# A Mamba-2 layer on one core: most input-projection tiles computed in pairs, by seven half-size products, with weight sums made by accumulating DMA

## The chip, the core and the metric

The kernel runs on one core of one Trainium2 chip. The metric is the device time of one execution, in microseconds (us). TensorE (PE) multiplies matrices, VectorE (DVE) and ScalarE (ACT) do elementwise work, GpSimd (POOL) and SyncE (SP) are used here to issue DMAs. Each engine runs its own instructions in the order in which they stand in the program, and waits where an instruction needs something that another engine or a DMA has not finished.

## What is computed

With DEPTH = 1 the reference is one layer, the Mamba-2 mixer, between two RMSNorms, on 512 tokens of 2048 channels in float32:

```python
proj = rmsnorm(x, ln_g) @ w_in        # 2048 -> 4096 z | 4096 x | 1024 B | 1024 C | 64 dt
z, xbc, dt = split(proj)
xs, bm, cm = split(silu(causal_depthwise_conv(xbc, conv_w, conv_b)))
dt = softplus(dt + dt_bias); a = -exp(a_log)
y = ssd_chunked_scan(xs * dt, dt * a, bm, cm) + d_skip * xs    # 64 heads of 64, 8 groups, state 128
y = rmsnorm(y * silu(z), norm_g) @ w_out
out = rmsnorm(x + y, final_g)
```

## The kernel before

**The input projection.** The 10240 output channels (without dt) are 80 tiles of 128 channels. One tile is a sum over 16 blocks of 128 input channels, for all 512 tokens at once. Weights and x are each split into two float32r parts, hi and lo, and each block takes three matmuls: hi times xh, hi times xl, lo times xh (mm_k, L175 to L179). So a tile is 48 matmuls of 128x512. A tile's weights come in two halves of 512 KB: SP issues the load (load_piece, L72), ACT casts the half to hi (L80), DVE subtracts to get lo (L81). The loaded halves rotate through two buffers ("raw"), the split ones through three ("hi", "lo").

**The order of the work.** The list seq (L102) puts the tiles in order: B and C of a group of heads, then x and z of each "unit" u (two heads, one tile of x and one of z; 32 units, four to a group). PE, SP and here also the events follow the order in which the program writes them; DVE and ACT instructions are put in order by a scheduler when the kernel is built. The scan's work is written as events at fixed steps of the projection, one step for each block of a tile (the tables usual and ramp, L532 to L534): u_load fetches a unit's decay sums, broadcast over 128 partitions, into csb (512 KB); u_decay (L420) makes from them the masked decay matrix m on ACT and DVE; u_xt transposes xs on PE; u_state makes the state of two units; u_yd (L482) multiplies m and x on PE; u_yo (L506) adds the part from the state, multiplies by silu(z) and stores y.

**After a tile.** When an x tile is done, DVE multiplies it by the token's norm into xr (L361), makes the four taps of the convolution (L363, three times L366), and ACT applies SiLU (L368). When a z tile is done, DVE multiplies by the norm (L502) and ACT applies SiLU (L503). The sums are in PSUM tiles named mm, of which there are two, so PE goes on with the next tile while these are read.

**The output projection** (L619 to L722) follows, 1536 matmuls of 128x512; it reads y back from DRAM.

The functions that the change touches:

Of the kernel before, what the change touches and what calls it, by code (L numbers as in the profile page):

```python
# [10 lines left out]
F32 = mybir.dt.float32  # L11
# [4 lines left out]
MANUAL = {mybir.EngineType.PE, mybir.EngineType.SP}  # L16
# [12 lines left out]
EPS = 1e-6  # L29


@with_exitstack
def mamba_layer(ctx: ExitStack, tc: tile.TileContext, d: dict, out: bass.AP):
# [7 lines left out]
    yp0 = ctx.enter_context(tc.tile_pool(name="yp0", bufs=1))  # L41
# [9 lines left out]
    xp = phx.enter_context(tc.tile_pool(name="xhat", bufs=1, side="right"))  # L51
    ps_tr = ph1.enter_context(psum("ps_tr", 2))
    ps_yd = ph1.enter_context(psum("ps_yd", 1))
    ps_yo = ph1.enter_context(psum("ps_yo", 1))
    ps_st = ph1.enter_context(psum("ps_st", 1))
# [16 lines left out]
    def load_piece(src, shape):  # L72
        raw = wp.tile(shape, F32, name="raw", bufs=2)
        nc.sync.dma_start(raw, src)
        return raw

    def split_piece(raw, shape, pool):
        hi = pool.tile(shape, F32R, name="hi")
        lo = pool.tile(shape, F32R, name="lo")
        S.copy(out=hi, in_=raw)  # L80
        V.tensor_tensor(out=lo, in0=raw, in1=hi, op=ALU.subtract)  # L81
        return hi, lo
# [19 lines left out]
    seq = [("B", 0), ("C", 0)]  # L102
    for u in range(NU):
        if u % UPG == 2 and u + 2 < NU:
            seq += [("B", u // UPG + 1), ("C", u // UPG + 1)]
        seq += [("x", u), ("z", u)]
    tile_of = {"z": 0, "x": 32, "B": 64, "C": 72}
    at = {s: i for i, s in enumerate(seq)}
# [9 lines left out]
    NP = 2 * len(seq)  # L118
    pieces = {}

    def w_src(n):
        kind, i = seq[n // 2]
        return d["wi"][tile_of[kind] + i, :, (n % 2) * 8:(n % 2) * 8 + 8, :]

    def get_piece(n):
        if n in pieces or n >= NP + len(wo_order):
            return
        if n < NP:
            pieces[n] = split_piece(load_piece(w_src(n), WSH), WSH, wp)
        else:  # L130
            p, s = wo_order[n - NP]
            pieces[n] = split_piece(load_piece(wo_src(p, s), OSH), OSH, op if n % 4 == 3 else wp)


    xh = [xp.tile([P, L], F32R, name=f"xh{k}") for k in range(KT)]
    xl = [xp.tile([P, L], F32R, name=f"xl{k}") for k in range(KT)]
    xr = sp.tile([P, L + 3], F32, name="xr")

    xbuf = [("csb", 2), ("csb", 2), ("m", 2), ("msh", 1), ("msl", 1)]

    def load_x(k2):
        name, bufs = xbuf[k2 % 5]
        raw = sp.tile([P, 2, L], F32, name=name, bufs=bufs)
# [5 lines left out]
    def split_x(k2, raw):  # L149
        for j in range(2):  # L150
            k = 2 * k2 + j
            S.activation(xh[k], raw[:, j, :], AF.Identity, scale=lng[:, k:k + 1])
            V.scalar_tensor_tensor(out=xl[k], in0=raw[:, j, :], scalar=lng[:, k:k + 1],
                                   in1=xh[k].bitcast(F32), op0=ALU.mult, op1=ALU.subtract)
# [4 lines left out]
    sqbuf = [(n, 2) for n in ("xs", "bc", "y", "z", "csth", "cstl") for _ in range(2)] + \  # L159
        [(n, 1) for n in ("bsl", "bsh")] + [("xd", 2), ("xdth", 2)]  # L160

    def square_x(k2, raw):
        for j in range(2):
            name, bufs = sqbuf[2 * k2 + j]
            sq = sp.tile([P, L], F32, name=name, bufs=bufs)
            S.activation(sq, raw[:, j, :], AF.Square)
            sqs.append(sq)
# [7 lines left out]
    def mm_k(ps, w, k8, k):  # L175
        hi, lo = w
        T.matmul(ps, hi[:, k8, :], xh[k], start=k == 0, stop=False)  # L177
        T.matmul(ps, hi[:, k8, :], xl[k], start=False, stop=False)  # L178
        T.matmul(ps, lo[:, k8, :], xh[k], start=False, stop=k == KT - 1)  # L179


    ps_bc = ps_yd.tile([P, 2, L], F32, name="yd")
    w0, raws, xraw = {}, {}, {}

    def bc_raw(t, half):
        raws[t, half] = wp.tile(WSH, F32, name="raw", bufs=2)
        pool, a, b = (yp0, "yh", "yl") if t and half else (wp, "hi", "lo")
# [570 lines left out]
```

## Time and profile before

| | before |
|---|---|
| median of 3 runs | 1374.59 us (1374.23 to 1374.94) |
| the profiled execution, its time | 1374.24 us |
| its span | 1372.5 us, so 1.7 us lie around the span |
| busy: PE, DVE, ACT, POOL | 1355.7, 876.7, 626.6, 1.7 us |
| DMA: moved, queue of SP and ACT | 170.85 MB, 38.4% of 16 engines' span |

In the page's groups, a row gives line, engine, operation, what is written from what, the shape, the count, then busy time in us, mean ns of one instruction, and the idle time of the engine before them. A matmul's duration contains its way through the array and overlaps the next one, so the distance from one start to the next, in the timeline, is what a matmul costs in a row of them. In the timeline a row is start, duration, engine, line, operation; consecutive equal instructions are merged.

### The profile page before, as it was taken

To read this page: it belongs to the slowest core of one execution; us is meant where nothing else is said; L and a number is where in the kernel's file an instruction comes from. 1 tells how busy PE (TensorE), PEld (TensorE's weight loads), DVE (VectorE), ACT (ScalarE), POOL (GpSimd) and SP (SyncE) were. 2 spreads that over 40 slices of the span, in tenths; PEclk is the share of its full clock that TensorE was granted. 3 is DMA by queue.
4 is the path that set the end of the run, shared out by engine and by line. 5 is a ranking of instruction groups with operands and counts; after the bars stand their busy time and mean duration, and the time that the engine had idled before them with its cause. 6 is when DMAs were issued, how large, how long until landed. Compare 5 with 4: busy or idle time off the path is not lost.

```text
span 1372.5 us, 16466 instructions
## 1 busy us (share of the span) xinstructions
PE 1355.7 (99%) x6388; PEld 1097.1 (80%) x6388; DVE 876.7 (64%) x1433; ACT 626.6 (46%) x894; POOL 1.7 (0%) x11
## 2 busy tenths in 40 slices
PE   7999999999999999999999999999999999999997
PEld 5888878888888888888878888888888888888885
DVE  7867665765666575666557665667647665566545
ACT  7455653635465273546346443736453222223213
POOL 0000000000000000000000000000000000000000
PEclk9999999999999999999999999999999999999998
DMA  7333443523433252434324343424444445454402
GB/s 235 94 113 104 146 126 98 160 58 131 130 112 115 77 158 87 150 100 133 107 77 161 97 134 102 147 92 131 128 146 145 146 152 169 146 163 147 137 30 93
DMA packets 55182, 170.85 MB, mean 124 GB/s; under 512 B 6720, under 2 KB 11136, under 8 KB 54976
## 3 DMA queue, kind: packets, MB, share of 16 engines
q1 hardware_dynamic: 54384, 167.95, 38.4%
q10 hardware_dynamic: 720, 1.84, 0.4%
q8 instruction: 50, 0.82, 0.2%
q14 instruction: 28, 0.23, 0.1%
HBM read 156.99 MB, written 12.78 MB: 124 GB/s over the span
## 4 chain that ended last, share of the span: by engine, by line
PE 97%; DMA 1%; DVE 0%; SPq 0%; ACT 0%; issue 0%; DVEq 0%; ACTq 0%
PE mm L177 21%; PE mm L179 21%; PE mm L178 21%; PE mm L630 9%; PE mm L629 9%; PE mm L631 9%; PE yd L489 2%; DMA raw<-in_wi 1%; PE yd L493 1%; PE tr L456 1%; PE st L477 1%; PE yo L381 0%; PE yo L380 0%; PE yo L382 0%; PE tr L299 0%; PE tr L381 0%
## 5 line engine op out<-in xcount | busy, mean ns | idle before, releaser
L177 PE MATMUL mm<-xh,hi 128*128 128x512 f32 x1248 | 497.1, 398 | 0.0
L179 PE MATMUL mm<-xh,lo 128*128 128x512 f32 x1248 | 489.0, 392 | 0.0
L178 PE MATMUL mm<-xl,hi 128*128 128x512 f32 x1248 | 488.6, 392 | 0.0
L81 DVE TENSOR_TENSOR lo<-raw,hi 128x1024 fp32r<-128x1024 f32 x212 | 258.8, 1221 | 151.8 <-ACT hi L80 151.6
L80 ACT CAST hi<-raw 128x1024 fp32r<-128x1024 f32 x212 | 220.9, 1045 | 262.9 <-PE mm L178 108.6
L179 PEld LDWEIGHTS mm<-xh,lo 128*128 128x128 f32 x1248 | 234.4, 188 | 52.5
L177 PEld LDWEIGHTS mm<-xh,hi 128*128 128x128 f32 x1248 | 234.6, 188 | 51.7 <-issue 5.3
L178 PEld LDWEIGHTS mm<-xl,hi 128*128 128x128 f32 x1248 | 234.7, 188 | 46.2
L630 PE MATMUL mm<-lo,yh 128*128 128x512 f32 x512 | 201.9, 394 | 0.0
L629 PE MATMUL mm<-hi,yh 128*128 128x512 f32 x512 | 201.7, 394 | 0.0
L631 PE MATMUL mm<-hi,yl 128*128 128x512 f32 x512 | 201.7, 394 | 0.0
L629 PEld LDWEIGHTS mm<-hi,yh 128*128 128x128 f32 x512 | 96.2, 188 | 23.2 <-ACT acc L682 0.6
L631 PEld LDWEIGHTS mm<-hi,yl 128*128 128x128 f32 x512 | 96.1, 188 | 22.4
L630 PEld LDWEIGHTS mm<-lo,yh 128*128 128x128 f32 x512 | 96.1, 188 | 22.2
L519 ACT ACTIVATE z<-y 128x512 f32<-128x512 f32 x31 | 19.6, 633 | 123.5 <-DVE y L513 123.5
L686 DVE SCALAR_TENSOR_TENSOR acc<-mm,ry,acc 128x512 f32<-128x512 f32 x72 | 53.4, 747 | 30.5 <-PE mm L631 29.6
L366 DVE SCALAR_TENSOR_TENSOR xs<-xr,par,xs 128x512 f32<-128x512 f32 x96 | 71.8, 748 | 1.4
L436 ACT ACTIVATE m<-csb,cs 128x128 f32<-128x128 f32 x128 | 47.1, 391 | 51.4 <-DMA csb<-cscr 38.1
L442 DVE TENSOR_TENSOR m<-m,cbm 128x512 f32<-128x512 f32 x64 | 44.1, 689 | 38.5 <-ACT m L439 24.2
L368 ACT ACTIVATE xs<-xs 128x512 f32<-128x512 f32 x32 | 20.2, 632 | 69.2 <-DVE xs L366 69.2
L438 DVE TENSOR_SCALAR m<-csb,cs 128x128 f32<-128x128 f32 x128 | 33.7, 280 | 24.5 <-DMA csb<-cscr 24.4
L458 DVE TENSOR_TENSOR xd<-tr,dt 128x512 f32<-128x512 f32 x32 | 22.0, 687 | 31.3 <-PE tr L456 31.3
(211 smaller groups left out, 1173.2 us busy)
## 6 DMA issues: line engine op xcount, KB each, us to landing
raw<-in_wi SPq DMA_DIRECT2D x158, 512.0 KB, 3.9
raw<-in_wo SPq DMA_DIRECT2D x64, 512.0 KB, 4.1
csb<-cscr SPq DMA_DIRECT2D x32, 512.0 KB, 5.8
yscr<-y SPq DMA_DIRECT2D x32, 256.0 KB, 2.3
yr<-yscr SPq DMA_DIRECT2D x16, 512.0 KB, 4.7
ecs<-escr SPq DMA_DIRECT2D x64, 64.0 KB, 5.4
xt<-in_x SPq DMA_DIRECT2D x16, 256.0 KB, 4.6
csb<-in_xT SPq DMA_DIRECT2D x3, 512.0 KB, 8.9
```

The source lines that it names most:

```text
L80: S.copy(out=hi, in_=raw)
L81: V.tensor_tensor(out=lo, in0=raw, in1=hi, op=ALU.subtract)
L177: T.matmul(ps, hi[:, k8, :], xh[k], start=k == 0, stop=False)
L178: T.matmul(ps, hi[:, k8, :], xl[k], start=False, stop=False)
L179: T.matmul(ps, lo[:, k8, :], xh[k], start=False, stop=k == KT - 1)
L366: V.scalar_tensor_tensor(out=ca, in0=xr[:, k:k + L], scalar=convw[:, t, k:k + 1], in1=ca, op0=ALU.mult, op1=ALU.add)
L436: S.activation(o, l, AF.Relu, scale=-1.0, bias=b)
L442: V.tensor_tensor(out=ma[:, i], in0=ma[:, i], op=ALU.mult, in1=cbm[:, i, 0:2, :].rearrange("p b l -> p (b l)").unsqueeze(1).to_broadcast([ ...
L629: T.matmul(ps, yh, hi, start=k == 0, stop=False)
L630: T.matmul(ps, yh, lo, start=False, stop=False)
L631: T.matmul(ps, yl, hi, start=False, stop=k == n - 1)
L686: V.scalar_tensor_tensor(out=a, in0=ps, scalar=ry[:, t:t + 1], in1=a, op0=ALU.mult, op1=ALU.add)
```

## The change

Four pairs of tiles (B and C of group 0, x and z of units 0 and 1, B and C of group 1) stay as they were. The other 36 pairs, p = x or B and q = z or C, are computed together, by a scheme of Winograd's kind with seven products in place of eight. The two tiles' weights are four halves by input channels; x is four quarters, by input channels and by tokens. A product is 8 blocks of three matmuls of 128x256 (product, L584), so a pair takes 168 matmuls of 128x256 in place of 96 of 128x512.

- **Weights.** Four halves are loaded as before (R11, R12, R21, R22). Four sums are made by DMAs that POOL issues and that add a half from DRAM onto a half in the chip's memory (q_add, L558): T1 is made on top of R11, T2 on top of T1, T4 on top of T2, all three in one buffer ra; T3 on top of R12 in buffer rb. Each sum can start when the split of what stood there has been read by ACT and DVE. All seven are split into hi and lo by ACT (L81) and DVE (L82), R11 into buffers of its own (h1h, h1l), the other six through three buffers. R21 and R22 use two buffers rc.
- **x.** Four sums of quarters of x are made once, on the chip: three forms in x_forms from a second load of x, in buffers s0 to s11, and one in x_form3 over the second half of the tokens of the first 8 blocks.
- **Products of a pair** (pair, L595), in order: R11 into S, T4 of the pair before into A, T1 into R, R21 into A, T2 onto S, R22 onto R, T3 onto S. S and R are PSUM tiles, of which a pair uses one half and the next pair the other. A is the tile of p; the tile of q comes out of S and R with sign changed. Between products ACT copies S or R away (L605, L609, L612, L617), and DVE adds the copies to R and S for z (L614, L616). T4's product, written in the next pair, ends p; then DVE does norm and convolution as before (L374, L365, three times L368).
- **The units.** Their events now stand at 28 steps to a pair, a step for every 6 matmuls. m and csb have one buffer in place of two, xd too. u_decay makes all its sums on ACT (8 Relu and 4 Exp of 128x128, one Exp of 128x1024) and one product on DVE (L436, 128x1536). The state is made unit by unit by two float32 matmuls (L462) in place of six float32r ones for two units; B, C and the scan's mask are no longer split where they make the decay's mask (L408, L409: float32).

```diff
+    NPL = 8
...
+    QS = 28
...
+        m = sp.tile([P, 2, 6, P], F32, name="m")
...
-                for o, l, b in ((ma[:, i, hh, 0:P], la, cs[:, 2 * i, h:h + 1]),
...
-                    if i == 0:
-                        S.activation(o, l, AF.Relu, scale=-1.0, bias=b)
-                    else:
-                        V.tensor_scalar(out=o, in0=l, scalar1=b, scalar2=0.0, op0=ALU.subtract, op1=ALU.min)
...
+                S.activation(m[:, i, hh, :], la, AF.Relu, scale=-1.0, bias=cs[:, 2 * i, h:h + 1])
+                S.activation(m[:, i, 2 + hh, :], lb, AF.Relu, scale=-1.0, bias=cs[:, 2 * i + 1, h:h + 1])
+                S.activation(m[:, i, 4 + hh, :], lb, AF.Exp, bias=nwl[:, 2 * i, h:h + 1])
+        S.activation(m[:, :, 0:4, :], m[:, :, 0:4, :], AF.Exp, scale=-1.0)
+        m6 = m.rearrange("p c (b h) l -> p (c b) h l", h=2)
+        V.tensor_tensor(out=m6, in0=m6, op=ALU.mult,
+                        in1=cbm.rearrange("p c b l -> p (c b) l").unsqueeze(2).to_broadcast([P, 6, 2, P]))
...
-        xd = sp.tile([P, NC, 2, HD], F32, name="xd", bufs=2)
+        xd = sp.tile([P, NC, 2, HD], F32, name="xd")
...
-        pst = ps_st.tile([P, 4 * HD], F32, name="st")
...
-        terms = [(Bt[0], xw[0]), (Bt[0], xw[1]), (Bt[1], xw[0])]
+        pyo = ps_yo.tile([P, 3, P], F32, name="yo")
...
         for c in range(2):
-            for i, (a, b) in enumerate(terms):
-                T.matmul(pst, a[:, c, :], b[:, c].rearrange("p u h d -> p (u h d)"), start=c + i == 0, stop=c + i == 3)
-        st = split(pst, [P, 4 * HD], "sts")
...
+            T.matmul(pyo[:, 2, :], Bt[:, c, :], xw[:, c].rearrange("p h d -> p (h d)"), start=c == 0, stop=c == 1)
+        un[u]["sts"] = split(pyo[:, 2, :], [P, P], "sts")
+        un[u]["pyo"] = pyo
...
+            S.copy(out=hi, in_=t)
+            V.tensor_tensor(out=lo, in0=t, in1=hi, op=ALU.subtract)
+
+        V.tensor_tensor(out=t1, in0=n2[:, :, hi_], in1=n1[:, :, hi_], op=ALU.subtract)
+        V.scalar_tensor_tensor(out=t2, in0=t1, scalar=-1.0, in1=n1[:, :, lo_], op0=ALU.mult, op1=ALU.subtract)
+        put(1, t1)
+        V.scalar_tensor_tensor(out=t1, in0=t2, scalar=-1.0, in1=n2[:, :, lo_], op0=ALU.mult, op1=ALU.subtract)
+        put(2, t2)
+        put(4, t1)
+
...
+    def q_split(n, f, own=False):
+        raw = qs[n][f]
+        qs[n, f] = split_piece(raw, WSH, wp, *((("h1h", "h1l"), 1) if own else ()))
...
+    def q_add(n, f, old, half, tile_):
+
+        raw = qs[n][old]
+        nc.gpsimd.dma_start(raw, w_half(quads[n][tile_], half), accum_op=ALU.add)
+        qs[n][f] = raw
...
+    def q_events(n):
+        b = NPL * KT + n * QS
+        for o, f, a in ((-34, q_load, ("R11", 0, 0, "ra")), (-15, q_split, ("R11", True)),
+                        (-15, q_add, ("T1", "R11", 0, 1)), (-2, q_split, ("T1",)),
+                        (-2, q_add, ("T2", "T1", 1, 1)), (13, q_split, ("T2",)),
+                        (13, q_add, ("T4", "T2", 1, 0)), (24, q_split, ("T4",)),
+                        (-7, q_load, ("R12", 0, 1, "rb")), (-6, q_add, ("T3", "R12", 1, 1)),
+                        (21, q_split, ("T3",)),
+                        (-10, q_load, ("R21", 1, 0, "rc")), (1, q_split, ("R21",)),
+                        (2, q_load, ("R22", 1, 1, "rc")), (17, q_split, ("R22",))):
+            add(b + o, f, n, *a)
...
+    def product(ps, w, f, first, step):
...
+        for k in range(KH):
+            if k % 2 == 0:
+                run(step + k // 2)
+            hi, lo = w()
+            ah, al = operand(f, k)
+            T.matmul(ps, hi[:, k, :], ah, start=first and k == 0, stop=False, skip_group_check=True)
+            T.matmul(ps, hi[:, k, :], al, start=False, stop=False, skip_group_check=True)
+            T.matmul(ps, lo[:, k, :], ah, start=False, stop=k == KH - 1, skip_group_check=True)
...
+    def pair(n, prev):
...
+        A = ps_mm.tile([P, L], F32, name="mm")
+        s_, r_ = [x[:, (n % 2) * LH:(n % 2) * LH + LH] for x in SR]
...
+        product(s_, W("R11"), 11, True, b)
+        S.copy(out=A[:, lo_], in_=s_)
+        if prev:
+            prev(b + 4)
+        product(r_, W("T1"), 1, True, b + 8)
+        S.copy(out=sn[:, 1, :], in_=r_)
+        product(A[:, lo_], W("R21"), 12, False, b + 12)
+        product(s_, W("T2"), 2, False, b + 16)
+        S.copy(out=sn[:, 0, :], in_=s_)
+        product(r_, W("R22"), 4, False, b + 20)
+        V.tensor_tensor(out=zq[:, lo_], in0=r_, in1=sn[:, 0, :], op=ALU.add)
+        product(s_, W("T3"), 3, False, b + 24)
+        V.tensor_tensor(out=zq[:, hi_], in0=s_, in1=sn[:, 1, :], op=ALU.add)
+        S.copy(out=A[:, hi_], in_=s_)
...
+            V.tensor_tensor(out=zq, in0=zq, in1=rbc, op=ALU.mult)
+            S.activation(zq, zq, AF.Silu, scale=-1.0)
...
+        def last(step):
+            product(A[:, hi_], W("T4"), 22, False, step)
+            normed(A)
+            (g_b if kp == "B" else u_x)(ip)
...
+    ramp = [[57, 62, 54, 73, 84, 90], [48, 57, 48, 66, 82, 88]]
...
+        w = ramp[u] if u < len(ramp) else [24, 38, 50, 58, 61, 66]
+        for o, f in zip(w, (u_load, u_decay, u_xt, u_state, u_yd, u_yo)):
+            add(at["x", u] + o, f, u)
...
+    nc = bacc.Bacc("TRN2", target_bir_lowering=False, num_devices=1, dynamic_dma_scratch_size=1024)
```

**Order, PE at the seam of two tiles or pairs.** Before, the end of one tile (xh_121 is the last block of x) and the start of the next; names in brackets are the semaphores of the engines waited for:

```order
L380 MATMUL yo<-csth,stsh 128x256 [waits DVE_49]
L381 MATMUL yo<-cstl,stsh 128x256
L382 MATMUL yo<-csth,stsl 128x256
L177 MATMUL mm<-xh_121,hi 128x512
L178 MATMUL mm<-xl_137,hi 128x512
L179 MATMUL mm<-xh_121,lo 128x512
L177 MATMUL mm<-xh_106,hi 128x512
L178 MATMUL mm<-xl_122,hi 128x512
L179 MATMUL mm<-xh_106,lo 128x512
```

Now, the end of T3's product and the start of the next pair's R11 product, both in S:

```order
L592 MATMUL S<-xl,hi 128x256
L593 MATMUL S<-xh,lo 128x256
L591 MATMUL S<-xh,hi 128x256
L592 MATMUL S<-xl,hi 128x256
L593 MATMUL S<-xh,lo 128x256
L591 MATMUL S<-xh,h1h 128x256 [waits Activation_49]
L592 MATMUL S<-xl,h1h 128x256
L593 MATMUL S<-xh,h1l 128x256
L591 MATMUL S<-xh,h1h 128x256
L592 MATMUL S<-xl,h1h 128x256
L593 MATMUL S<-xh,h1l 128x256
```

Before, the next tile starts here with no wait of its own. Now the first matmul of the next pair waits for an ACT instruction, the copy L617 of the sum that has just ended.

**Order, ACT around the end of a pair.** Before, the stretch around a z tile (L503); L368 and L439 belong to the same and the next unit:

```order
L439 ACT_TABLE_LOAD
L439 ACTIVATE m<-m 128x768
L440 ACTIVATE m<-m 128x768
L80 CAST hi<-raw 128x1024
L368 ACT_TABLE_LOAD
L368 ACTIVATE xs<-xs 128x512
L80 CAST hi<-raw 128x1024 x2
L503 ACTIVATE z<-z 128x512
L466 CAST xwsh<-xw 128x2x128
L374 CAST stsh<-st 128x256
L80 CAST hi<-raw 128x1024
```

Now, the splits of T4, of the next pair's T1 and R21 (ra, ra, rc), then the copy L617 that PE waits for, SiLU of z and the split of the state:

```order
L612 COPY sn<-S 128x256
L81 CAST hi<-ra 128x1024 x2
L81 CAST hi<-rc 128x1024
L617 COPY mm<-S 128x256
L623 ACTIVATE z<-z 128x512
L379 CAST stsh<-yo 128x128
L81 CAST h1h<-ra 128x1024
L605 COPY mm<-S 128x256
```

Where before only a weight split and SiLU stood, a copy that PE waits for now stands behind three weight splits, and the first two of these read what accumulating DMAs have written.

**Order, DVE from the end of an x tile to the next weight split.** Before:

```order
L361 TENSOR_TENSOR xr<-mm,rbc 128x512
L438 TENSOR_SCALAR m<-csb,nwl 128x128
L363 TENSOR_SCALAR xs<-xr,par 128x512
L81 TENSOR_TENSOR lo<-raw,hi 128x1024
L366 SCALAR_TENSOR_TENSOR xs<-xr,par,xs 128x512
L438 TENSOR_SCALAR m<-csb,cs 128x128
L366 SCALAR_TENSOR_TENSOR xs<-xr,par,xs 128x512
L438 TENSOR_SCALAR m<-csb,cs 128x128
L366 SCALAR_TENSOR_TENSOR xs<-xr,par,xs 128x512
```

Now, from the end of T4's product (L374) to the split of T2 (L82 lo<-ra):

```order
L374 TENSOR_TENSOR xr<-mm,rbc 128x512
L365 TENSOR_SCALAR xs<-xr,par 128x512
L368 SCALAR_TENSOR_TENSOR xs<-xr,par,xs 128x512
L492 TENSOR_TENSOR ecs<-yo,ecs 128x256
L368 SCALAR_TENSOR_TENSOR xs<-xr,par,xs 128x512
L493 TENSOR_TENSOR y<-y,ecs 128x256
L368 SCALAR_TENSOR_TENSOR xs<-xr,par,xs 128x512
L494 TENSOR_TENSOR y<-y,z 128x512
L436 TENSOR_TENSOR m<-m,cbm 128x1536
L82 TENSOR_TENSOR lo<-ra,hi 128x1024
```

Before, a weight split stands fourth. Now all of the convolution, the unit's y (L492 to L494) and the whole decay product (L436) stand ahead of the split of T2.

More of the change, by code (lines that the diff above doesn't have):

```diff
@@ L29 @@
 EPS = 1e-6
+KH = KT // 2
+LH = L // 2
 @with_exitstack
@@ L598, in mamba_layer @@
     add(b0 + 56, dt_spread)
-    for n in range(2, len(seq)):
+    for n in range(2, NPL):
         ps = None
@@ L614, in mamba_layer @@
             finish(n, ps)
+    prev = None
+    SR = [ps_q.tile([P, L], F32, name=x) for x in ("S", "R")]
+    for n in range(len(quads)):
+        prev = pair(n, prev)
+    prev(END)
     phx.close()
-    assert NP + 3 not in pieces
     op = ctx.enter_context(tc.tile_pool(name="op", bufs=1, side="right"))
     acc = [op.tile([P, DM], F32, name=f"acc{t}") for t in range(NC)]
-    step = len(seq) * KT
+    step = END + 4
     def mm_o(ps, blk, w, t):
```

314 lines of the change are left out of this document (169 added, 145 removed).

## Prediction

> **What bounds the kernel now.** I read the page first: the busy times and the chain that ended last.
>
> ```profile
> PE 1355.7 (99%) x6388; PEld 1097.1 (80%) x6388; DVE 876.7 (64%) x1433; ACT 626.6 (46%) x894; POOL 1.7 (0%) x11
> PE 97%; DMA 1%; DVE 0%; SPq 0%; ACT 0%; issue 0%; DVEq 0%; ACTq 0%
> ```
>
> PE is busy for 99% of the span and is 97% of the chain. Then the waits, for PE alone:
>
> ```profile
> PE yd L177 <- ACT xh L152: 6.4, 1, 6.4
> PE yd L178 <- DVE xl L153: 1.1, 3, 0.6
> ```
>
> These are all: 7.5 us, at the start. Every result of DVE, ACT and DMA is there before PE wants it. So a matmul fewer is time gained, as long as that stays so; and a wait that PE gets is time lost in full. Third, the timeline of PE, for what a matmul costs in a row of them: 21 matmuls of 128x512 between the first two rows, six of 128x256 between the next three.
>
> ```profile
> 600.59 0.40 PE L177 MATMUL mm<-xh,hi 128*128 128x512 f32 x1
> ...
> 605.40 0.39 PE L177 MATMUL mm<-xh,hi 128*128 128x512 f32 x1
> ...
> 662.48 0.28 PE L477 MATMUL st<-xwsh,bth 128*128 128x256 f32 x1
> ...
> 663.07 0.28 PE L477 MATMUL st<-xwsh,btl 128*128 128x256 f32 x1
> ...
> 663.19 0.40 PE L177 MATMUL mm<-xh,hi 128*128 128x512 f32 x1
> ```
>
> A 128x512 costs 4.81 / 21 = 0.2290 us. The last of the six 128x256 starts at 663.07 and the next matmul at 663.19, so one costs 0.71 / 6 = 0.1183 us: a little more than half.
>
> **Part 1, the products.** 36 pairs had 36 x 96 = 3456 matmuls of 128x512, 791.4 us. They get 36 x 168 = 6048 of 128x256, 715.5 us. Gain: 75.9 us, not the eighth (98.9) that the count of products promises, since the half-size matmul is dearer by its share. The Trainium skill's page "TensorE: Matmul & The Clock Gate" (Back-to-back issue gap) gives N/2.4 + 2.5 ns, 216 and 109 ns; by that the gain would be 85 us. The trace has 229 and 118 ns, and decides.
>
> **Part 2, the scan on PE.** The state took six 128x256 for two units, 0.71 us. It takes four float32 128x128. For these the nearest row is L275, four such matmuls in eight records:
>
> ```profile
> L275 PE MATMUL tr<-z,ones x8: 270/275/276, 45.3 to 46.1; 128*128 128x128 f32 x8
> 642.09 0.28 PE L380 MATMUL tr<-csth,bsh 128*128 128x256 f32 x1
> 643.42 0.45 PE L177 MATMUL mm<-xh,hi 128*128 128x512 f32 x1
> 631.03 0.60 PE L456 MATMUL tr<-ident,xs 128*128 128x128 f32 x4
> 631.39 0.48 PE L177 MATMUL mm<-xh,hi 128*128 128x512 f32 x1
> ```
>
> 0.8 / 7 is 0.114 us a record, 0.23 a matmul, 0.91 for two units: 0.2 more, 16 times, +3.3 us. The decay's mask took twelve matmuls, 1.33 us from 642.09 to 643.42; two float32 of 256 and two of 128 columns come to 2 x (0.46 + 0.23) = 1.37: nothing. The four transposes of xs keep their 0.36 us.
>
> **Part 3, the split of T2 behind the decay.** Prices on DVE and ACT, from the groups (mean ns behind the busy time):
>
> ```profile
> L81 DVE TENSOR_TENSOR lo<-raw,hi 128x1024 fp32r<-128x1024 f32 x212 | 258.8, 1221 | 151.8 <-ACT hi L80 151.6
> L80 ACT CAST hi<-raw 128x1024 fp32r<-128x1024 f32 x212 | 220.9, 1045 | 262.9 <-PE mm L178 108.6 <-PE mm L631 92.8 <-DMA raw<-in_wi 34.6
> L361 DVE TENSOR_TENSOR xr<-mm,rbc 128x512 f32<-128x512 f32 x46 | 31.5, 685 | 15.2 <-PE mm L179 15.0
> L363 DVE TENSOR_SCALAR xs<-xr,par 128x512 f32<-128x512 f32 x32 | 17.4, 544 | 0.6
> L366 DVE SCALAR_TENSOR_TENSOR xs<-xr,par,xs 128x512 f32<-128x512 f32 x96 | 71.8, 748 | 1.4
> L511 DVE TENSOR_TENSOR ecs<-yo,ecs 128x256 f32<-128x256 f32 x32 | 13.5, 421 | 30.1 <-PE yo L382 30.0
> L512 DVE TENSOR_TENSOR y<-y,ecs 128x256 f32<-128x256 f32 x32 | 13.4, 420 | 0.6
> L513 DVE TENSOR_TENSOR y<-y,z 128x512 f32<-128x512 f32 x32 | 22.0, 688 | 0.6
> L442 DVE TENSOR_TENSOR m<-m,cbm 128x512 f32<-128x512 f32 x64 | 44.1, 689 | 38.5 <-ACT m L439 24.2 <-ACT m L440 14.1
> L436 ACT ACTIVATE m<-csb,cs 128x128 f32<-128x128 f32 x128 | 47.1, 391 | 51.4 <-DMA csb<-cscr 38.1 <-PE tr L382 9.2 <-PE mm L178 4.1
> L439 ACT ACT_TABLE_LOAD x27 | 34.6, 1283 | 0.5
> L439 ACT ACTIVATE m<-m 128x768 f32<-128x768 f32 x32 | 27.1, 845 | 0.3
> L374 ACT CAST stsh<-st 128x256 fp32r<-128x256 f32 x16 | 5.9, 371 | 50.0 <-PE st L477 50.0
> ```
>
> And how instructions follow each other, from the timeline:
>
> ```profile
> 610.56 0.85 ACT L439 ACTIVATE m<-m 128x768 f32<-128x768 f32 x1
> 611.32 1.98 ACT L80 CAST hi<-raw 128x1024 fp32r<-128x1024 f32 x2
> 611.44 0.69 DVE L442 TENSOR_TENSOR m<-m,cbm 128x512 f32<-128x512 f32 x1 [0.23 <-ACT m L439]
> 612.72 1.22 DVE L81 TENSOR_TENSOR lo<-raw,hi 128x1024 fp32r<-128x1024 f32 x1
> 613.85 0.74 DVE L366 SCALAR_TENSOR_TENSOR bc<-xr,par,bc 128x512 f32<-128x512 f32 x1
> ```
>
> An engine that waited starts 0.03 us after the end it waited for (610.56 + 0.85 = 611.41, L442 at 611.44). Instructions that don't need each other overlap by 0.09 (L81 would end at 613.94, the next starts at 613.85). Two weight casts take 1.98, so a cast follows after 0.94.
>
> When T4's last matmul starts, call it 0; it ends at 0.28 (the length of a 128x256 above), and DVE starts L374 at 0.31. In the new order ten instructions end with T2's lo: 0.685 + 0.544 + 3 x 0.748 + 0.421 + 0.420 + 0.688 + 1.75 + 1.221 = 7.97 us. (1.75 is L436 on 1536 elements: 0.689 for 512, 1.221 for 1024, so 0.53 for each further 512.) Seven overlaps take 0.63 off, two dependent starts add 0.06: 7.4 us, so lo is there at 7.75. PE meanwhile has T1's 24 matmuls, 3 for the state's part of y, R21's 24, and two of T2 that want only hi: it wants lo at 54 x 0.1183 = 6.39. **It waits 1.36 us a unit; 30 units, +40.8 us.** ACT's line to the same split is level: from the end of the unit's y on PE, 12 x 0.368 (47.1 / 128) + 1.28 + 1.06 (1024 elements) + 0.37 + 1.05 = 8.2 us, against 69 matmuls, 8.2 us. I add nothing for it.
>
> **Part 4, the seam between pairs.** Call the start of T3's last matmul 0. R21's cast waits for the matmul before it and starts at -0.12 + 0.28 + 0.03 = 0.19. L617 stands behind it: 1.13. It takes 0.37 (as L374), so PE may go on at 1.53; it could have at 0.12. **1.41 us at each of 35 seams, +49.4 us.** Were no cast in front, the line over L616 on DVE (as L511) would still give 0.31 + 0.42 + 0.03 + 0.37 + 0.03 = 1.16, a wait of 1.04, +36.4 us. The copies L605, L609 and L612 cost nothing: at least 24 other matmuls (2.84 us) stand between a product and the next use of its half of S, R or A, and 0.31 + 0.37 hides there.
>
> **Part 5, the adds.** No accumulating DMA and no DMA of POOL is in the trace. The nearest rows:
>
> ```profile
> q1 hardware_dynamic: 54384, 167.95, 38.4%
> raw<-in_wi SPq DMA_DIRECT2D x158, 512.0 KB, 3.9
> csb<-cscr SPq DMA_DIRECT2D x32, 512.0 KB, 5.8
> ```
>
> 167.95 MB in 38.4% of 1372.5 us is 319 GB/s, 1.64 us for 512 KB of data; 2.26 of the 3.9 us are not data. POOL issues T4's add when T2's lo is there, and the next pair's T1 add right behind it. T1's cast stands ahead of R21's cast and L617, so it has to start 0.94 us before R21's can. PE has from T2's third matmul 22 + 24 + 24 matmuls and the transposes, 8.64 us; so T1 must have landed within 7.7 us or the seam gets longer by all that it is late. Lower bound, adds like loads: 3.9 + 1.64 = 5.5, no cost. Upper bound: three times the data (read two, write one), 2.26 + 2 x 4.92 = 12.1. I take twice the data, since an add reads two sources where a load reads one: 2.26 + 2 x 3.28 = 8.8, and 0.8 for half of a load of SP (R21's, 1.64) among it: 9.6, late by 1.9. **35 x 1.9 = +66.5 us.** The Trainium skill's page "Collectives: The Full Stack" (the bandwidth ceiling) says this of adds by DMA: both sources go through one read ring, so a reduce runs at half a copy's rate; no run here shows it. That is the rule that speaks against this change.
>
> SP's R11 load waits for T4's lo, and behind it are csb and R22. csb's 5.8 us have until the next unit's decay, which waits for the unit's y on PE, over 6 us after T3: covered, barely. DMA's share: 144 adds of 3.28 us on 527 make 1000 us of some 1465, 68%: no bound.
>
> **Part 6, the forms of x.** DVE gets 40 instructions of 0.7 us, 28 us, in the stage that has the least room:
>
> ```profile
> 50.00:150.00 100.00, 100.00 (x482) 81.31 (x482) 77.20 (x142) 53.59 (x82) 0.00 (x0) 1.00 0.32 104
> ```
>
> DVE had 23 us idle of 100 there. I add 8, between 0 (spread) and 16.
>
> **The sum**, against the profiled span: 1372.5 - 75.9 + 3.3 + 40.8 + 49.4 + 66.5 + 8 = 1464.6; with the 1.7 us around it, 1466.3. The profiled execution took 1374.24, the median is 1374.59: the same for this purpose. About 0.2% (2.7 us) can be told from no change.
>
> **The rivals.**
>
> 1. *The adds land in time* (0.22). Then Part 5 is 0: 1399.8 us. For it: the loads' 5.5 us are under 7.7. The Trainium skill's "DMA: Bandwidth & Descriptors" (Anatomy of one DMA) has 2.0 us + bytes/436 GB/s for a DMA of GpSimd, an estimated 3.2 us for 512 KB, and so this time.
> 2. *The adds are slow* (0.13): with three times the data and the same 0.8, T1 lands after 12.9, 5.2 late: +182 in place of +66.5, 1581.8 us. Nothing in the profile excludes it.
> 3. *Faster* (0.12): DVE's line before T2 is hidden (it would have to end 1.4 us sooner, by more overlap), the adds are in time, and a seam costs only 1.04: 1372.5 - 75.9 + 3.3 + 36.4 + 8 + 1.7 = 1346.0 us. It decides from a total wait under (75.9 - 3.3 - 8) / 35 = 1.85 us a pair. Against it: Parts 3 and 4 alone sum to 2.6, from rows.
> 4. *Waits and gain cancel* (0.03).
>
> **How the numbers follow.** My forecast has 0.50; rivals 0.22, 0.13, 0.12, 0.03. Faster 0.12, same 0.03, slower 0.85. The range 1385 to 1580 holds the forecast and rival 1 with the bounds of Parts 5 and 6, and about half of rival 2; some 0.2 is outside.
>
> **What would show it.** In the profile after: matmuls of the products 0.118 us apart; waits of PE for ACT L617 of about 115 us in all (50 if the adds are in time) and for DVE L82 of about 40; POOL's adds 5 to 8 us from issue to landing; PE busy near 90%. Waits of PE under 65 us in all would make it wrong towards faster; adds over 10 us, towards rival 2; a PE that waits for ACT L81 more than for L617 would mean that the casts, not the seam, are the bound.

## The result, and the profile after the change

The changed kernel takes **1574.79 us** (median of 4 runs, 1569.62 to 1575.99), the kernel before 1374.72 in the same rounds: 1.1449 times as long, interval 1.1422 to 1.1475. The forecast was 1466.3 us in a range of 1385 to 1580. The sign and the range held; of the loss of 200 us the forecast had 92.

The page of the profile after, from the parts that were shown of before:

```profile
span 1567.9 us, 22414 instructions
PE 1355.0 (86%) x8980; PEld 1224.6 (78%) x8980; DVE 983.6 (63%) x1333; ACT 787.8 (50%) x1291; POOL 126.5 (8%) x155
q0 software_dynamic: 20736, 75.51, 26.6%
DMA 40%; PE 28%; issue 16%; DVE 9%; ACT 6%; POOL 1%; SPq 0%; POOLq 0%; ACTq 0%; DVEq 0%
```

PE was 97% of the chain that ended last; now DMA is 40% of it and PE 28%. PE's busy time is the same as before (1355.7), though the matmuls have 76 us less to do: that is the first sign that they ran slower. The mean clock granted to PE is 0.949 of full speed, before it was 0.997. POOL's adds, a median from issue to landing in the last column:

```profile
ra<-in_wi POOLq DMA_DIRECT2D x108, 512.0 KB, 8.5
```

The waits (in total, times, longest): PE's, which were 7.5 us in all before, and ACT's casts, which wait for the adds:

```profile
PE S L591 <- ACT mm L617: 106.5, 35, 5.8
PE S L593 <- DVE lo L82: 40.0, 30, 2.9
PE tr L408 <- DVE xd L450: 21.1, 7, 3.1
ACT hi L81 <- DMA ra<-in_wi: 192.9, 73, 3.9
```

With the smaller ones PE's sum to 203.3 us.

One seam, from the timelines of POOL, ACT, DVE and PE:

```profile
616.44 0.86 POOL L561 DMA_DIRECT2D ra<-in_wi  x1 [0.91 <-DVE h1l L82]
624.14 1.04 ACT L81 CAST hi<-ra 128x1024 fp32r<-128x1024 f32 x1 [2.85 <-DMA ra<-in_wi]
625.10 1.04 ACT L81 CAST hi<-rc 128x1024 fp32r<-128x1024 f32 x1
626.81 0.36 ACT L617 COPY mm<-S 128x256 f32<-128x256 f32 x1 [0.68 <-DVE z L616]
625.22 1.22 DVE L82 TENSOR_TENSOR lo<-ra,hi 128x1024 fp32r<-128x1024 f32 x1 [1.41 <-ACT hi L81]
626.36 0.42 DVE L616 TENSOR_TENSOR z<-S,sn 128x256 f32<-128x256 f32 x1
623.74 0.28 PE L593 MATMUL S<-xh,lo 128*128 128x256 f32 x1
627.22 0.58 PE L591 MATMUL S<-xh,h1h 128*128 128x256 f32 x1 [3.20 <-ACT mm L617]
627.60 0.41 PE L592 MATMUL S<-xl,h1h 128*128 128x256 f32 x1
627.82 0.41 PE L593 MATMUL S<-xh,h1l 128*128 128x256 f32 x1
...
630.65 0.28 PE L592 MATMUL S<-xl,h1h 128*128 128x256 f32 x1
630.77 0.28 PE L593 MATMUL S<-xh,h1l 128*128 128x256 f32 x1
```

T1's add is issued at 616.44 and lands 7.7 us later. Its cast, R21's cast and T1's lo follow, L616 stands on DVE behind that lo, L617 behind L616, and PE goes on at 627.22, after 3.2 us. That is the forecast's seam. What the forecast didn't have is behind it: the matmuls come 0.21 us apart where 0.12 is usual, until 630.2. The windows of the same stretch (PE, weight loads, DVE, ACT and POOL busy, then the granted clock):

```profile
626.00:628.00 2.00, 0.78 (x3) 0.78 (x4) 1.97 (x4) 0.95 (x3) 1.50 (x2) 0.71 0.86 251
628.00:630.00 2.00, 2.00 (x12) 2.00 (x11) 0.64 (x1) 0.17 (x1) 0.00 (x0) 0.50 0.97 305
630.00:632.00 2.00, 2.00 (x18) 2.00 (x18) 0.29 (x1) 0.27 (x1) 0.00 (x0) 0.94 1.08 241
```

Half the clock from about 626.8 until 630.2 (0.71 and 0.94 are windows that hold both), so for some 3 us of PE's work: 12 matmuls in 2 us where 18 follow in the next two.

How much that is in all: the forecast's terms without any wait give 1372.5 - 7.5 - 75.9 + 3.3 + 8 = 1300.4 us, the **base**. With the 203.3 us of waits that is 1503.7. The span is 1567.9. The **rest**, 64.2 us, is in neither matmuls at full pace nor waits. An estimate from PE's rows alone agrees: this trace has 153.6 us at half clock amid its work, and the distances between matmuls there exceed the usual ones by 64 us in all. The theory to test (A): the waits have the causes that the forecast named, and behind a wait of several us PE's clock is halved, which costs the rest. The rivals: the rest comes from the products or the adds' traffic (B); or the adds are no cause at all and only the order on ACT is.

### The profile page after: what moved, and what is told of

It reads as the page before. It is cut to its first block, busy times and chain, and to the rows that moved or that the text cites. A ratio compares the mean times of both kernels' runs of the same rounds, so it can differ in the third digit from the quotient of the medians.

```text
span 1567.9 us, 22414 instructions
## 1 busy us (share of the span) xinstructions
PE 1355.0 (86%) x8980; PEld 1224.6 (78%) x8980; DVE 983.6 (63%) x1333; ACT 787.8 (50%) x1291; POOL 126.5 (8%) x155
## 3 DMA queue, kind: packets, MB, share of 16 engines
q0 software_dynamic: 20736, 75.51, 26.6%
## 4 chain that ended last, share of the span: by engine, by line
DMA 40%; PE 28%; issue 16%; DVE 9%; ACT 6%; POOL 1%; SPq 0%; POOLq 0%; ACTq 0%; DVEq 0%
DMA ra<-in_wi 34%; PE mm L750 7%; PE mm L751 7%; PE mm L749 7%; DVE lo L82 4%; ACT hi L81 3%; DMA rb<-in_wi 3%; DMA csb<-cscr 1%; DVE xs L368 1%; DMA ra<-in_wo 1%; POOL ra L561 1%; PE mm L180 1%; PE mm L181 1%; PE mm L182 1%; PE S L591 1%
## 5 line engine op out<-in xcount | busy, mean ns | idle before, releaser
L81 ACT CAST hi<-ra 128x1024 fp32r<-128x1024 f32 x168 | 176.1, 1048 | 342.2 <-DMA ra<-in_wi 192.9
L82 DVE TENSOR_TENSOR lo<-ra,hi 128x1024 fp32r<-128x1024 f32 x168 | 205.1, 1222 | 204.8 <-ACT hi L81 200.2
L591 PE MATMUL S<-xh,h1h 128*128 128x256 f32 x288 | 104.5, 363 | 106.5 <-ACT mm L617 106.5
L591 PE MATMUL mm<-xh,hi 128*128 128x256 f32 x576 | 163.7, 284 | 2.2 <-ACT mm L617 2.2
L593 PE MATMUL R<-s,lo 128*128 128x256 f32 x576 | 161.1, 280 | 2.9 <-DVE lo L82 2.9
L591 PE MATMUL R<-s,hi 128*128 128x256 f32 x576 | 163.4, 284 | 0.0
L593 PE MATMUL mm<-xh,lo 128*128 128x256 f32 x576 | 160.4, 278 | 3.4 <-DVE lo L82 3.4
L592 PE MATMUL mm<-xl,hi 128*128 128x256 f32 x576 | 160.6, 279 | 0.0
L592 PE MATMUL R<-s,hi 128*128 128x256 f32 x576 | 160.4, 278 | 0.0
L591 PEld LDWEIGHTS mm<-xh,hi 128*128 128x128 f32 x576 | 108.2, 188 | 7.2 <-issue 4.8
L591 PEld LDWEIGHTS R<-s,hi 128*128 128x128 f32 x576 | 108.2, 188 | 0.0
L592 PEld LDWEIGHTS R<-s,hi 128*128 128x128 f32 x576 | 108.2, 188 | 0.0
L592 PEld LDWEIGHTS mm<-xl,hi 128*128 128x128 f32 x576 | 108.1, 188 | 0.0
L81 ACT CAST hi<-rc 128x1024 fp32r<-128x1024 f32 x76 | 79.2, 1042 | 39.3 <-PE S L592 25.2
```

The lines of the kernel that those rows point to most:

```text
L591: T.matmul(ps, hi[:, k, :], ah, start=first and k == 0, stop=False, skip_group_check=True)
L592: T.matmul(ps, hi[:, k, :], al, start=False, stop=False, skip_group_check=True)
L593: T.matmul(ps, lo[:, k, :], ah, start=False, stop=k == KH - 1, skip_group_check=True)
```

## The experiments

Below, the rest of a run is its span less 1300.4 less the sum of PE's waits.

### Plain loads for the adds

```
-        nc.gpsimd.dma_start(raw, w_half(quads[n][tile_], half), accum_op=ALU.add)
+        nc.gpsimd.dma_start(raw, w_half(quads[n][tile_], half))
```

> The 144 adds of POOL become plain loads of the same 512 KB from the same queue at the same places (the sums of weights are not made: the products take the second tile alone). Theory A (the adds are late, and PE's clock falls after waits of several us): a load of 512 KB takes 5 to 6 us instead of 8.5, so T1 lands in time; PE's wait for L617 falls from 106 to about 50 us, that for L408 and L593 stays, and of the 70 us of lowered clock some 20 go: about 1494 us. Rival B (the adds cost nothing at the seam, the order of casts on ACT does): L617's wait stays above 95 us, 1560 to 1575 us.

Measured: **1457.23 us** (1.0603, 1.0585 to 1.062), clock 0.986. PE's waits, and then POOL's DMAs on the page:

```profile
PE S L591 <- ACT mm L617: 55.6, 35, 2.9
```

```profile
q0 software_dynamic: 20736, 75.51, 15.1%
ra<-in_wi POOLq DMA_DIRECT2D x108, 512.0 KB, 5.3
```

L617's wait falls from 106.5 to 55.6: the late adds are 50.9 us of it, the seam by itself 55.6. The waits are 130.8 us in all, 72.5 less than with adds, but the time is 118 less: the rest falls from 64.2 to 18.4 us with it (1449.6 - 1300.4 - 130.8). So A was right on the wait, and its time is 37 us too long: more of the lost clock came back than it had. No wait at L617 is over 3 us any more. Of the 35 seams, 21 now wait 1.29 us, the least that any has; with the adds 12 wait 1.29 to 1.39, and 20 wait 2.4 to 5.8: the adds make some seams much longer and others not at all. The same 75.51 MB take 15.1% of 1449.6 us, 345 GB/s; as adds 26.6% of 1567.9, 181 GB/s.

### S and R change roles from pair to pair

```
-        s_, r_ = [x[:, ...] for x in SR]
+        s_, r_ = [x[:, ...] for x in SR[::1 - n % 2 * 2]]
```

> S and R change roles from pair to pair, so that the next pair's R11 goes to the tensor that L614 has read long before, and no longer waits for L617; T4 of the pair before wants L617 24 matmuls (2.84 us) later. Theory A: of 106.5 us behind L617 (35 waits, 3.0 each) some 15 stay, in front of T4's first matmul; the clock is lowered less, by some 35 us: 1445 us. Rival B (the late add of T1 sets the pace, whatever waits for it): the wait moves to T4 or T1 nearly whole, over 80 us of it, 1545 us or more.

Measured: **1484.23 us** (1.0802, 1.0786 to 1.0818), clock 0.967. All of the computation is kept.

```profile
PE tr L408 <- DVE xd L450: 21.9, 7, 4.2
PE R L593 <- DVE lo L82: 21.0, 20, 1.3
PE S L593 <- DVE lo L82: 19.0, 19, 1.5
PE R L591 <- ACT hi L81: 13.9, 4, 5.9
PE mm L591 <- ACT mm L617: 9.4, 9, 2.4
```

Of L617's 106.5 us, 9.4 stay, so the late copy mattered mainly because the very next product wanted the tensor that it reads. Some of the wait moved: R11's product now waits 14.1 us for L614, and T2's 23.2 for its cast (L81), which was 5.6. The time is 39 us over what A expected: the waits that are left sum to 138.0, with 5.9 and 4.2 us among the longest, and the rest is still 43.2.

### Waits put into the kernel before

This is the test of the clock by itself: the kernel before, all of its work, and two small POOL instructions that the first matmul of a tile must wait for.

```
+    def hold(src, w):
+        dl = sp.tile([P, 1], F32, name="dl", bufs=2)
+        Q.tensor_scalar(out=dl, in0=src[:, 0:1], scalar1=0.0, scalar2=1.0, op0=ALU.mult, op1=ALU.add)
+        Q.tensor_tensor(out=w, in0=w, in1=dl, op=ALU.mult)
...
+            if n > 9 and k == 0 and seq[n - 1][0] == "x":
+                hold(un[seq[n - 1][1]]["xs"], pieces[2 * n][0][:, 0, 0:1])
```

In a first form the two POOL instructions were copies that didn't need each other.

> The kernel before, all of its work, with 29 to 32 waits added: the first matmul after each x tile waits for a POOL copy that waits for the unit's x (conv and silu), some 5 us. Theory A (the clock falls after such waits): the granted clock falls from 0.997 to 0.95 or less, matmuls after a wait are over 0.3 us apart for some us, and the span grows by clearly more than the waits, by 30 to 80 us. Rival B (the lowered clock of the changed kernel comes from its products or its traffic): clock 0.99 or more, and the span grows by the waits alone, to within 10 us.

> As the one with long waits, but the first matmul after each z tile waits for the gate z (one instruction of DVE and one of ACT), some 2 us. Theory A (only waits of several us lower the clock): clock 0.99 or more, the span grows by the waits alone. Theory C (any wait of PE lowers it): clock under 0.98, and the span grows by the waits and 20 us or more.

These two tell nothing of it: the scheduler put the second copy ahead of the first, and PE waited for neither. They took 1386.59 and 1388.23 us at a clock of 0.998. In the form above:

> The kernel before with all of its work, and 29 waits of PE added: the first matmul of the tile behind an x tile waits for two small POOL instructions, and these for the unit's x (conv and silu on DVE and ACT), some 5 us; this time the second POOL instruction needs the first one's result, so that the scheduler can't put it ahead. Theory A (the granted clock falls after a wait of 2.5 us or more, and 1.5 to 3 us are lost behind each): clock 0.96 or less, and the span grows by the waits and 45 to 90 us more. Rival B (the lowered clock comes from the products or the traffic of the adds): clock 0.99 or more, and the span grows by the waits to within 10 us.

> The same behind z tiles, where the two POOL instructions wait for the gate z, one instruction of DVE and one of ACT, so about 2 us. Theory A (a wait under 2 us costs 0.3 to 0.5 us beside itself, a longer one 1.5 and more): clock 0.98 or more, and the span grows by the waits and some 10 to 20 us. Rival C (any wait lowers the clock alike): clock and added time as with the long waits.

> The kernel before with the waits behind the gate z, but at the third k of the tile, two k steps (1.4 us) later, so that 117.6 us of waits become some 75, most of them 1.2 to 1.6 us. Theory A (under 2 us the clock stays): clock 0.98 or more, no more than 15 us beside the waits themselves. Rival C (any wait of this kind costs 1.6 us beside itself): 45 us beside the waits.

Measured, one run each: **1641.51 us** behind x, **1539.02** behind z, **1482.78** behind z two steps later; clock 0.930, 0.961, 0.977. PE's waits for POOL in the three, in this order:

```profile
PE mm L177 <- POOL hi L526: 202.6, 29, 10.3
```

```profile
PE mm L177 <- POOL hi L526: 117.6, 29, 7.0
```

```profile
PE mm L177 <- POOL hi L526: 77.1, 29, 5.8
```

The spans grew by 267.3, 164.8 and 108.6 us, so by 64.7, 47.2 and 31.5 more than these waits: 2.2, 1.6 and 1.1 us a wait. Some 5 us of each surplus are not the clock: a wait is counted from the end of the last matmul's record (0.39 us), while without a wait the next one would start 0.23 us after its start, so each of the 29 costs 0.16 us more than is counted. No product was changed and no add was there, so B falls. A's numbers held behind x alone: behind z it had 10 to 20 us (the waits are 4.1 us on the mean, not 2), and two steps later 15 at most. Then waits of different length, first one of the third kernel and after it three of the second, each with the matmuls behind it:

```profile
723.68 0.50 PE L177 MATMUL mm<-xh,hi 128*128 128x512 f32 x1 [1.33 <-POOL hi L526]
724.02 0.40 PE L178 MATMUL mm<-xl,hi 128*128 128x512 f32 x1
724.26 0.39 PE L179 MATMUL mm<-xh,lo 128*128 128x512 f32 x1
```

```profile
672.04 0.50 PE L177 MATMUL mm<-xh,hi 128*128 128x512 f32 x1 [2.70 <-POOL hi L526]
672.38 0.40 PE L178 MATMUL mm<-xl,hi 128*128 128x512 f32 x1
672.62 0.39 PE L179 MATMUL mm<-xh,lo 128*128 128x512 f32 x1
...
608.84 0.51 PE L177 MATMUL mm<-xh,hi 128*128 128x512 f32 x1 [2.70 <-POOL hi L526]
609.18 0.40 PE L178 MATMUL mm<-xl,hi 128*128 128x512 f32 x1
609.42 0.50 PE L179 MATMUL mm<-xh,lo 128*128 128x512 f32 x1
609.72 0.63 PE L177 MATMUL mm<-xh,hi 128*128 128x512 f32 x1
610.14 0.63 PE L178 MATMUL mm<-xl,hi 128*128 128x512 f32 x1
...
723.69 0.80 PE L177 MATMUL mm<-xh,hi 128*128 128x512 f32 x1 [3.59 <-POOL hi L526]
724.28 0.63 PE L178 MATMUL mm<-xl,hi 128*128 128x512 f32 x1
724.71 0.63 PE L179 MATMUL mm<-xh,lo 128*128 128x512 f32 x1
```

Behind 1.33 us the matmuls are 0.24 apart from the second on. Behind 3.59 they are slow at once (0.59 from the first start to the second, then 0.43 apart). Behind two waits of the same 2.70 us it goes both ways. Read so over the stretch from 200 to 1160 us of these two kernels: the 15 waits of 1.33 to 2.2 us lost 0.5 us or less behind them; of 14 of 2.5 to 2.7 us eight lost 1.3 to 2.0 and six nothing; of the 23 longer ones all but one lost 1.6 to 3.1, no more for 7 us than for 4. So rival C, that any wait costs alike, falls too.

But the length of a wait doesn't decide it by itself. Ahead of that stretch a wait of 2.15 us (second kernel, at 142 us) and one of 2.29 us (third kernel, at 169 us) lost 1.3 and 1.7 us. What decides is in the clock that the traces record. In every trace here it changes only at moments that are whole steps of 3.41 us apart. These are the windows of the second kernel cut at those moments, around the two waits of 2.70 us that end at 608.84 and 672.04 (length, PE, weight loads, DVE, ACT and POOL busy, then the clock):

```profile
606.15:609.56 3.41, 0.72 (x3) 0.62 (x4) 2.52 (x5) 1.75 (x3) 1.02 (x2) 1.00 0.00 0
609.56:612.97 3.41, 3.41 (x10) 2.64 (x9) 0.00 (x0) 0.00 (x0) 0.00 (x0) 0.50 0.00 0
...
667.58:671.00 3.42, 1.76 (x10) 1.14 (x8) 2.25 (x4) 1.81 (x3) 0.11 (x1) 1.00 0.14 56
671.00:674.41 3.41, 2.37 (x10) 1.99 (x11) 0.94 (x2) 0.09 (x1) 0.90 (x2) 1.00 0.01 2
674.41:677.82 3.41, 3.41 (x19) 2.91 (x18) 0.00 (x0) 0.00 (x0) 0.00 (x0) 1.00 0.00 0
```

The first wait lies whole in one step, and the next step is at half clock. The second is cut by the end of a step into 1.66 and 1.04 us, and no fall comes. Counted over every step of full clock in the changed kernel and in the second and third kernel here (the first 12 and the last 15 us left out): each of the 66 falls comes after a step with 1.7 us of waiting or more, and none of the 1156 other steps has over 1.9. Two waits in one step add up. In the changed kernel one of 0.88 and one of 0.85 us were enough:

```profile
903.31:906.72 3.41, 1.68 (x13) 1.27 (x12) 3.41 (x4) 2.44 (x3) 0.00 (x0) 1.00 0.02 2
906.72:910.13 3.41, 3.41 (x16) 3.41 (x17) 3.41 (x4) 3.38 (x5) 1.70 (x2) 0.50 0.43 55
```

So PE's clock is halved for the next step when about half of a step was idle. In the three kernels a fall lasts one step or two; a wait over 2.5 us often fills half a step, and one of 1.33 us can't by itself.

The Trainium skill's page "TensorE: Matmul & The Clock Gate" (Part 1: The HAM clock gate) describes this: a gate halves PE's clock when PE was idle over a window of about 3.4 us, the window runs freely, and while the gate is down matmuls of 512 columns are 426.7 ns apart. The 0.43 agrees, and so does the window that runs freely: steps of 3.41 us, and equal waits that go both ways. That PE has to be idle for all of it doesn't: 1.7 to 1.9 us of a step were enough here.

### Other places for the adds and the splits

On top of the change of roles, the steps at which splits and adds are issued:

```
-(-15, q_split, ("R11", True)), (-15, q_add, ("T1", "R11", 0, 1)),
+(-20, q_split, ("R11", True)), (-20, q_add, ("T1", "R11", 0, 1)),
-(-6, q_add, ("T3", "R12", 1, 1)),
+(3, q_add, ("T3", "R12", 1, 1)),
```

> S and R change roles, and POOL's adds are put in another order: R11's split and T1's add five steps sooner, ahead of T4's add of the pair before, and T3's add nine steps later, so that it no longer holds up T2's add on POOL's queue while it waits for R12 to land. Theory A (what is left of the waits is late T1 and T2, set by the queue's order): waits for ACT L81 and DVE L82 in the products fall from 65 to under 30 us, those for L450 stay at 20; 1484 less 35 of waits and 25 of clock: 1425 us. Rival B (DVE's line ahead of T2's lo, or the adds' bytes, hold them): they stay over 50 us, 1470 us.

Then, besides, `(13, q_split, ("T2",))` and T4's add moved to step 9, and `g_cb` from step 24 to 19:

> As the one with the other order of adds, and T2's split stands four steps sooner, ahead of the decay's multiplication on DVE, and the group's C by B (L408) five steps sooner, ahead of the unit's transposes, so that it doesn't want the transposes' PSUM tensor before DVE has read it. Theory A: the 20 us behind L450 go too, and T2's lo is in time: waits of some 25 us in all beside the ramp's, clock 0.99, about 1375 us. Rival B (ACT, which now waits for T2's add amid the decay, is late with everything behind it): waits for ACT over 40 us, 1430 us or more.

Measured: 1472.34 us (1.0711, 1.0693 to 1.0729) and **1384.03 us** (1.0072, 1.0056 to 1.0089). The order of the adds alone gives little, and its waits for DVE L82 stay at 46.5: there B was right, DVE's line ahead of T2's lo holds it. With that line shortened, these are PE's waits in the products, and L408's are gone:

```profile
PE R L593 <- DVE lo L82: 20.3, 14, 2.0
PE S L593 <- DVE lo L82: 15.4, 12, 2.4
```

All of PE's waits sum to 66.5, the rest to 13.6, at a clock of 0.982. T2's split and the C by B were moved in one run, so what each gives by itself isn't shown. Of the 200 us that the change lost, these four edits give 191 back, with every product and every add in place. Then R22's lo, the one that is still late (29.5 of the 35.7 us), was put ahead of the decay's multiplication: the decay at step 42 rather than 38, R22's split at 13 rather than 17; and the same with plain loads for the adds.

> As the one with everything (roles, order of adds, T2's split, C by B), and the decay four steps later and R22's split four steps sooner, so that R22's lo stands ahead of the decay's multiplication (1.75 us) on DVE. Theory A: the 36 us of PE behind DVE L82 go to under 12, and with them some 15 of the 25 us that the clock still takes: 1384 less 24 less 15, about 1345 us, under the kernel before. Rival B (the decay comes late for the unit's y, or ACT's casts wait for R22 to land): a new wait for DVE L436 or ACT L81 of 20 us or more, 1370 us or more.

> As the one with the decay later, but with plain loads in place of the 144 adds (the sums of weights are not made). Theory A (with the new order the adds are hidden): within 15 us of the same kernel with adds. Rival B (an add's 8.5 us to landing still hold the chain R11, T1, T2, T4): 25 us or more less.

Measured: 1388.55 us (1.0112, 1.0094 to 1.0129) and 1348.49 (0.9813, 0.9798 to 0.9829). The waits for L82 went from 36 to 15 us, but others came for L370 and L612, and all of PE's sum to 65.9 as against 66.5. With plain loads 45.4 us of waits are left and a rest of 3.8 (1349.6 - 1300.4 - 45.4): the base of 1300.4, the forecast's Parts 1, 2 and 6 taken together, comes out right to some 4 us. In this order the adds still cost 40 us, as B had it.

Five more runs looked for these 40 us, the second from the one with spread adds, the others from the one with the decay later.

> As the one with the decay later, and the adds spread evenly over the pair: T3's add six steps sooner, with R12's load and T3's split four steps sooner, so that T3 and T2 are no longer in flight together; T4's split three steps and R11's load five steps later. Theory A (two adds at once share the rate and land late, 10.7 us for T3's): T3's adds land in 8 us, PE's waits for ACT and DVE in the products fall by 15 us or more, about 1365 us. Rival B (ACT's order, in which a cast that waits for an add stands ahead of the copy L612 and the silu L370): those waits stay, 1380 us or more.

> As the one with spread adds, and ACT's instructions in the order in which the program is written rather than the scheduler's, with T2's split two steps sooner: so T4's cast, which waits for an add, stands behind the copy L612, and T3's behind the unit's silu. Theory A (a cast that waits for its add holds up what stands behind it on ACT): waits for L612 and L370 go, some 20 us with what the clock loses behind them, about 1350 us. Rival B (program order makes ACT wait elsewhere, for DVE's conv ahead of the silu): new waits of 20 us or more, 1380 us or more.

> As the one with the decay later, with one more number changed: for the third unit of a group the load of csb stands 18 steps sooner. In that unit the scheduler puts the decay's first instruction ahead of R11's cast on ACT, where it waits up to 3 us for csb to land, and behind it come, late one after the other, R11's lo, T1's add, T4's add beside it and T4's cast, which holds up the silu L370 and the copy L612. Theory A (this one load starts what is left of the seams): the waits for L370 and L612, 15.6 us, go, and some 25 us of lowered clock behind them; 1388 less 35, about 1350 us, under the kernel before. Rival B (the adds' time to landing does it wherever the decay stands): the waits for L612 and for casts stay at 10 us or more, 1375 us or more.

> As the one with the decay later, and csb's load of a group's third unit two steps sooner instead of 18, so just ahead of R11's load on SP's queue; in the order that the scheduler makes of it, the unit's silu L370 stands ahead of T3's cast and L612 ahead of T4's cast in this pair. Theory A (casts that wait for their add hold up the short instructions behind them; the load sets this order): the waits for L370 and L612, 15.6 us, go, and some 10 us of lowered clock: 1360 us, under the kernel before. Rival B (the adds' landing alone): as the one with the decay later, 1385 us.

> The same with the load four steps sooner: the silu stands ahead of T3's cast here too, but L612 behind T4's. Theory A: waits for L370 go, those for L612 (8.9 us) stay in part: about 1372 us. Rival B: 1385 us, as without it.

Measured: 1480.12, 1707.21, 1409.71, 1397.72 and 1390.53 us, none faster than the one it starts from; the last is level with it (1.0113 times the kernel before, as against 1.0112). With spread adds those of T1, T2 and T4 did land sooner (6.8 us rather than 7.6), but ACT then waited for R21's load. On SP's queue it had come to stand behind R12's, which waits for its one buffer until T3's lo is made (32 of the 33 waits), and L617 stands behind R21's cast on ACT:

```profile
ACT hi L81 <- DMA rc<-in_wi: 132.5, 33, 6.6
```

With ACT in program order PE waited 93.5 us for L81's casts and 43.9 for L410. Moving csb's load by 18, 2 or 4 steps took the waits for L370 away (1.2 us are left in the second) and put others in their place, for L614 (16.9 us), for L617 (14.6) and for L612 (17.4). No order that was tried has the adds hidden, and none was faster than the kernel before; that none could be isn't shown.

## Why the prediction was right in its parts, and the step that failed

- **Part 1, the products.** Right: at full clock the products' matmuls are 0.117 to 0.118 us apart. That the base holds to 4 us with plain loads is partly luck. That run has 34 us at half clock, an estimated 13.5 us lost, and 24 waits that each cost 0.16 us more than is counted, so its rest should be some 17 us: the base is some 14 too high. Part 6's 8 us are in it and came as a wait as well (6.7 us in that run for L661, which stands on DVE among the forms of x), and 0.001 us less a matmul makes some 6 on 6048. In the changed kernel the same base and some 95 waits cancel in the same way, so that the rest of 64.2 is the clock's.
- **Part 3, T2's lo.** 40.8 forecast, 40.0 measured in 30 waits. Right in place, count and size.
- **Part 4, the seam.** 49.4 forecast; with plain loads L617 costs 55.6 in 35 waits, 1.59 each as against 1.41. The least, 1.29, is 1.45 counted as the forecast counts, from where the next matmul would start: so the mechanism was right. In the seam shown the line is longer than the forecast's, since L616 stands behind T1's lo on DVE. The change of roles shows that most of the seam needn't exist.
- **Part 5, the adds.** 66.5 forecast, 106.5 - 55.6 = 50.9 measured. Mechanism right, size a little over on the mean. The forecast's 9.6 counts from the issue of T4's add; from there T1's land after 9.9 us on the mean, 9.2 (median) after their own issue. (The 5 to 8 us that the forecast gave as its sign don't fit its own sum; all adds have 8.5.) What it lacked is the spread: it made every seam late by 1.9, and 12 of 35 weren't late at all while others waited up to 5.8. That an add has half a load's rate (181 GB/s as against 345) agrees with the rule of the Trainium skill's page "Collectives: The Full Stack" (the bandwidth ceiling), by which it had been sized; rival 1, adds in time, was wrong by that.
- **The step that failed** is in the reading of before: "a wait that PE gets is time lost in full". When waits fill about half of a 3.41 us step, PE works at half clock in the next, so a wait of 2.5 us or more is mostly lost with 1.6 to 3 us on top. Seam and late add together are 3.0 us a pair on the mean, up to 5.8, and the clock fell 31 times: 64.2 us, the largest single error, which the forecast's sum has at nothing. The forecast had worked out 1.41 + 1.9 = 3.3 us a seam, and never asked what PE's clock does in it.
- **What wasn't listed:** 21.1 us at L408, which wants the transposes' PSUM tensor before DVE has read it; it wasn't costed. And smaller waits, 35.7 us in all where 7.5 of before were in the sum: 28.2, of which 6.0 are the wait for L661 that Part 6 had already.

Together: 64.2 + 21.1 + 28.2, less 9.4 at L617 (115.9 forecast) and 0.8 at T2, is 103.3, which is 1567.9 - 1464.6.

Rival 2 had nearly the measured time (1581.8) by the wrong mechanism: the adds were not slower than assumed. Rival 3 put the point of no loss at 1.85 us of wait a pair; with waits of 66.5 in all the mended kernel stands 10 us above the kernel before.

## What to carry to other kernels

Price a new wait of TensorE by its length and by the slow matmuls behind it: here the second was a third of the first (64.2 of 203.3 us). It came when waits filled about half of a 3.41 us step, so short waits that lie some steps apart cost less than one long, and two in the same step cost like one. When an accumulator's tensor is wanted again at once, exchange two such tensors from round to round before shortening the copy that empties it. A DMA that adds has to be issued earlier than a load (here it landed after 8.5 us rather than 5.3), and every cast that waits for it holds up what stands behind it on its engine.

## What the runs showed of the hardware

- PE's granted clock changed in steps of 3.41 us. It fell to 0.50 after a step with 1.7 to 1.9 us of waiting or more, from one wait or two; 512 columns then took 0.43 us a matmul rather than 0.23, for one step or two in most runs.
- In the longest waits the clock is down before PE resumes: with waits behind x, the window from 316 to 318 us, in which PE did nothing, has 0.51. So the mean granted clock of a run (0.930 there) overstates the loss, and the spacing of the matmuls has to be read instead.

```profile
316.00:318.00 2.00, 0.00 (x0) 0.00 (x0) 1.53 (x3) 0.37 (x1) 0.00 (x0) 0.51 0.73 201
```

- POOL's accumulating DMA of 512 KB landed in 8.5 us at 181 GB/s, the same DMA without accumulation in 5.3 at 345; SP's loads beside the adds took 5.7 to 7.1 us, beside the plain loads 4.7 to 6.0, and 3.9 before.
- The kernel before with POOL copies that PE never waited for took 12 to 14 us longer (1386.59 and 1388.23, one run each), at full clock. Over the whole trace its matmuls of 512 columns are 0.2326 us apart on the mean rather than 0.2301, which on 5400 of them makes some 13 us. Why isn't known; the three kernels whose PE waits for POOL have 0.230.
